# Output projection in a hybrid mixer kernel: from plain 128-token blocks to Strassen's seven products

## Chip, cores and metric

One core of a Trainium2 chip. The metric is the device time of one execution in microseconds (us); lower is better. Engines in the profile: PE is TensorE (PEld its weight loads), DVE is VectorE, ACT is ScalarE, POOL is GpSimd, SP is SyncE, which here only issues DMAs.

## What is computed

The reference is one layer of a diffusion backbone over 2,048 latent tokens and 256 context tokens with D_MODEL = 1024, all in fp32. Two token mixers (a bidirectional gated DeltaNet and a windowed attention) each give a 512-wide result per token, ya and yb. Then:

```
def _merge(ya, yb, ga, gb, w_proj_a, w_proj_b, w_out):
    y = jax.nn.sigmoid(ga) * (ya @ w_proj_a) + jax.nn.sigmoid(gb) * (yb @ w_proj_b)
    return y @ w_out
...
x = x + gate[:, None] * _merge(ya, yb, ga, gb, w_proj_a, w_proj_b, w_out)
```

The change is about the last product alone, y (2048 x 1024) by w_out (1024 x 1024), with its gated residual.

## The kernel before

**Products in three passes.** A matmul of the kernel works on fp32r tiles: a value is split into a high part (an ACT copy into an fp32r tile) and a low part (value minus high part, a subtraction on DVE or POOL). A product of two split operands is three matmuls, high x high, high x low and low x high, added up in PSUM. Every operand of every dense product thus costs one ACT operation and one subtraction.

**The stages before the end.** Input projections, convolutions, the DeltaNet's scan and the attention come first. `project(pool, wp, gi, ...)` (L1187 on) makes y for a group gi of 512 tokens: for each of 8 blocks of 128 columns two PSUM groups of 12 matmuls (L1198 to L1200) with ya and yb, an evaluation of the gate on DVE (L1206), a sum (L1208, on DVE for the last group, else on POOL), and a store of the block to the DRAM scratch `ysp[gi]`, transposed: [128 columns, k, 512 tokens]. The groups come in the order 1, 2, 0, 3. Groups 1, 2 and 0 run between pieces of the attention; group 3 runs alone after it. Its y tiles lie in the pool `proj`; the projection weights lie in the four 16 KB tiles of the pool hA (tags hh0, hl0, hh1, hl1).

**The output projection** (L1239 to L1303) takes half a group, 256 tokens, at a time: eight halves. `load_half` brings y in four pieces (L1249, issued on ACT's queue) and splits them on ACT (L1250) and DVE (L1251). w_out is loaded in 16 pieces of 128 x 512 (L1270) and split on ACT (L1271) and POOL (L1272). Its first NWO = 5 k slices have tiles in the pools p4r and p4 (opened when the attention's pools close, one at either end of the free space); the other three take the place of projection weights in hA, so they wait for `project` to end. For half 0 the four output blocks (2 token blocks x 2 column halves) are first accumulated over k = 0 to 4, then finished; later halves run block by block, 24 matmuls each. A block leaves PSUM in a DVE multiply by the gate row gbc (L1298); POOL (DVE for the last half) adds the residual x (L1299), and the rows are stored.

**What sets the order.** The program is written in sequence, and a scheduler orders each engine's instructions by priority (position in the program) as soon as they are ready in its own estimate of the time; on the chip every engine then runs its list in order. `tc.high_priority` moves the loads and splits for half 0 and for w_out ahead, to the priority of `project` of group 3. Tiles of a pool are given places in the order in which they are first asked for; a new tile on the place of an older one waits until that one's last user is done. [...]

**Pools and places.** Before the last stage the free space of a partition holds, from the low end, the attention's left pool (about 38 KB), `proj` (y high and y low in two buffers of 4 KB each, then two tb tiles of 2 KB, 20 KB in all), and at the high end the attention's right pool (46 KB). The last stage's p4 starts at the low end (56 KB) and p4r ends at the high end (44 KB).

Of the kernel before, what the change touches and what calls it, by code (L numbers as in the profile page):

```python
# [7 lines left out]
F32 = mybir.dt.float32  # L8
# [9 lines left out]
KT = D // 128  # L18
# [10 lines left out]
def f32(ap):  # L29
    return ap.bitcast(F32)  # L30
# [10 lines left out]
def _hybrid(ctx, tc, nc, V, S, G, T, ins, out, dbg, upto):  # L41
# [1197 lines left out]
    with tc.tile_pool(name="p4r", bufs=2, side="right", reuse_waits="tile") as pr4, \  # L1239
            tc.tile_pool(name="p4", bufs=2, reuse_waits="tile") as p4:  # L1240
        halves = [2 * gi + j for gi in (1, 2, 0, 3) for j in range(2)]

        def load_half(i):
            pool = pr4 if i % 2 == 0 else p4
            yh = pool.tile([128, KT, 256], F32R, name=f"yh{i % 2}", bufs=1)
            yl = pool.tile([128, KT, 256], F32R, name=f"yl{i % 2}", bufs=1)
            for k in range(0, KT, 2):
                yr = pr4.tile([128, 2, 256], F32, name="yq")
                adma(yr, ysp[halves[i] // 2][:, k:k + 2, halves[i] % 2 * 256:halves[i] % 2 * 256 + 256])  # L1249
                S.copy(yh[:, k:k + 2], yr)  # L1250
                V.tensor_tensor(yl[:, k:k + 2], yr, f32(yh[:, k:k + 2]), op=ALU.subtract)  # L1251
            return yh, yl

        woh, wol = [], []
        with tc.high_priority(tc.cur_priority - p_last):
            yy = load_half(0)
            for k in range(KT):
                if k < NWO:
                    pool = pr4 if k < 2 else p4
                    woh.append(pool.tile([128, D], F32R, name=f"woh{k}", bufs=1))  # L1260
                    wol.append(pool.tile([128, D], F32R, name=f"wol{k}", bufs=1))
                else:
                    if (k - NWO) % 2 == 0:
                        wo4 = hA.tile([128, 4, D], F32R, name="wo4", tag=("hh0", "hl0")[(k - NWO) // 2])
                    woh.append(wo4[:, (k - NWO) % 2 * 2])
                    wol.append(wo4[:, (k - NWO) % 2 * 2 + 1])
                for n in range(2):
                    ns = slice(n * 512, n * 512 + 512)
                    wr = pr4.tile([128, 512], F32, name="wor", bufs=4)
                    adma(wr, ins["w_out"][0, k * 128:(k + 1) * 128, ns])  # L1270
                    S.copy(woh[k][:, ns], wr)  # L1271
                    G.tensor_tensor(wol[k][:, ns], wr, f32(woh[k][:, ns]), op=ALU.subtract)  # L1272
        gbc = p4.tile([128, D], F32, name="gbc", bufs=1)
        dma(gbc, gsp.to_broadcast([128, D]))
        for i, hb in enumerate(halves):
            yh, yl = load_half(i) if i else yy
            tiles = [(tb, n, acc([128, 512], name="ops")) for tb in range(2) for n in range(2)]

            def products(tb, n, ps, ks):
                sl = slice(tb * 128, tb * 128 + 128)  # L1280
                ns = slice(n * 512, n * 512 + 512)
                for k in ks:
                    T.matmul(ps, lhsT=yh[:, k, sl], rhs=woh[k][:, ns], start=k == 0, stop=False)  # L1283
                    T.matmul(ps, lhsT=yh[:, k, sl], rhs=wol[k][:, ns], start=False, stop=False)  # L1284
                    T.matmul(ps, lhsT=yl[:, k, sl], rhs=woh[k][:, ns], start=False, stop=k == KT - 1)  # L1285

            if i == 0:
                for t in tiles:
                    products(*t, range(NWO))
# [59 lines left out]
```

## Time and profile before

| | |
|---|---|
| Median of 3 runs | 2045.72 us (2042.43 to 2046.54) |
| The profiled execution's own time | 2046.15 us |
| Its span, first to last instruction | 2044.3 us |
| Granted TensorE clock, mean | 0.988 |
| Output projection: first to last matmul | 1862.40 to 2039.93 us |
| DMA over the span | 333.12 MB, mean 163 GB/s |

The span is one profiled execution of the program; a line of it names the source line, the engine, the operation, the tiles written and read, and the count. "128x512" is partitions by elements. In a timeline the first two columns are start and duration in us, and "[1.15 <-DMA wor]" says that the engine was idle for 1.15 us before and what ended it; several instructions in a row are merged into one line with "x3". In lines by source the three numbers are the shortest, the median and the longest duration in ns. In the table of stretches each engine has its busy us and, in brackets, its instructions, and PEclk is the granted clock as a share of the full one. A line's second bar starts the idle time before the group.

### The profile page before, as it was taken

Reading aid. Unit: us, or ns where it says so; the run is one execution under the profiler, and the core shown is the slowest. Engines: PE = TensorE matmul, PEld = TensorE weight load, DVE = VectorE, ACT = ScalarE, POOL = GpSimd, SP = SyncE. Lnnn points to the kernel's source line nnn. Section 1 sums busy time; section 2 is a strip of 40 time slices with the busy share of each in tenths; the row PEclk is TensorE's granted clock in tenths of the full one; section 3 lists DMA queues with packets and bytes.
Section 4 is the critical chain, followed back from the end, with each engine's and each line's share of the span. In section 5 each row is a group of like instructions: output and inputs, shape, how many; then the busy total and the mean of one; then the engine's idle time right before and its main releaser. Section 6 shows DMA issues by size and latency. Waiting matters only on the chain. (4 is left out here: it accounts for less than half of the span.)

```text
span 2044.3 us, 32068 instructions
## 1 busy us (share of the span) xinstructions
PE 1966.8 (96%) x11043; PEld 1643.2 (80%) x11043; DVE 1421.5 (70%) x2715; ACT 760.4 (37%) x1927; POOL 742.9 (36%) x876
## 2 busy tenths in 40 slices
PE   6899999989999999999999999999989999999999
PEld 3888888778898677787788888878868888878887
DVE  6888766667766999999689655536577777753322
ACT  5655555544443211101122233325476556531100
POOL 2862211235553433224322234324256443442321
PEclk8999999999999999999999999999999999999999
DMA  7462236754447533437876787663456655355542
GB/s 256 141 166 85 89 97 165 188 149 155 147 136 197 154 109 111 132 98 220 201 218 205 221 244 214 185 207 116 129 165 204 185 167 158 120 174 189 185 144 93
DMA packets 375511, 333.12 MB, mean 163 GB/s; under 512 B 83832, under 2 KB 299184, under 8 KB 374708
## 3 DMA queue, kind: packets, MB, share of 16 engines
q1 hardware_dynamic: 347924, 288.59, 49.1%
q10 hardware_dynamic: 27424, 42.48, 5.9%
q8 instruction: 87, 1.43, 0.3%
q14 instruction: 76, 0.62, 0.1%
HBM read 220.28 MB, written 109.13 MB: 161 GB/s over the span
## 5 line engine op out<-in xcount | busy, mean ns | idle before, releaser
L523 PE MATMUL rps<-hh,wh 128*128 128x512 f32 x768 | 309.9, 404 | 10.1 <-DVE rt L811 5.2
L525 PE MATMUL rps<-hh,wl 128*128 128x512 f32 x768 | 310.3, 404 | 1.6 <-DVE wl L243 1.6
L524 PE MATMUL rps<-hl,wh 128*128 128x512 f32 x768 | 307.8, 401 | 0.0
L242 POOL TENSOR_SCALAR wh<-wr 128x512 fp32r<-128x512 f32 x120 | 104.7, 885 | 278.6 <-PE rps L524 105.8
L523 PEld LDWEIGHTS rps<-hh,wh 128*128 128x128 f32 x768 | 145.6, 190 | 47.1 <-POOL wh L242 4.9
L525 PEld LDWEIGHTS rps<-hh,wl 128*128 128x128 f32 x768 | 145.4, 189 | 35.1 <-DVE wl L243 2.4
L523 PE MATMUL lps<-hh,wh 128*128 128x512 f32 (+1 forms) x448 | 172.1, 384 | 0.3 <-ACT y L633 0.3
L524 PEld LDWEIGHTS rps<-hl,wh 128*128 128x128 f32 x768 | 145.8, 190 | 32.9
L525 PE MATMUL lps<-hh,wl 128*128 128x512 f32 (+1 forms) x448 | 171.1, 382 | 0.0
L524 PE MATMUL lps<-hl,wh 128*128 128x512 f32 (+1 forms) x448 | 171.1, 382 | 0.0
L562 DVE SCALAR_TENSOR_TENSOR cacc<-y,cw,cacc 128x512 f32<-128x512 f32 (+1 forms) x224 | 160.6, 739 | 14.3 <-ACT cacc L560 11.3
L809 ACT ACTIVATE rt<-rps 128x512 f32<-128x512 f32 x96 | 57.3, 597 | 287.5 <-PE rps L525 228.6
L909 DVE CUSTOM_DVE_ANT_0 pr<-sc,band,sk 128x640 f32<-128x640 f32 (+1 forms) x128 | 106.4, 863 | 42.5 <-PE sc L905 22.1
L937 DVE TENSOR_TENSOR pl<-pt,ph 128x512 fp32r<-128x512 f32 x156 | 105.0, 685 | 40.9 <-ACT ph L935 40.3
L935 ACT CAST ph<-pt 128x512 fp32r<-128x512 f32 x156 | 90.2, 585 | 111.7 <-PE pt L933 77.0
L748 DVE TENSOR_TENSOR N<-N,btmp 128x62 f32<-128x62 f32 (+30 forms) x124 | 123.7, 997 | 3.1
L746 DVE TENSOR_TENSOR btmp<-N 128x62 f32<-128x62 f32 (+30 forms) x124 | 119.2, 962 | 3.2
L919 POOL TENSOR_SCALAR pr<-pr,sm 128x640 f32<-128x640 f32 (+1 forms) x128 | 98.9, 793 | 57.1 <-DVE sm L917 44.5
L911 ACT ACTIVATE pr<-pr,sm 128x640 f32<-128x640 f32 (+1 forms) x128 | 104.0, 815 | 24.6 <-DVE sm L909 24.6
L1198 PE MATMUL pps<-yh,wph 128*128 128x512 f32 x256 | 105.1, 414 | 5.0 <-DVE tb L1206 2.0
L243 DVE TENSOR_TENSOR wl<-wr,wh 128x512 fp32r<-128x512 f32 x120 | 94.0, 796 | 18.1 <-POOL wh L242 17.9
L1199 PE MATMUL pps<-yl,wph 128*128 128x512 f32 x256 | 101.7, 397 | 0.9 <-DVE yl L1181 0.9
(301 smaller groups left out, 4925.9 us busy)
## 6 DMA issues: line engine op xcount, KB each, us to landing
wr<-in_w_in_dram SPq DMA_DIRECT2D x120, 256.0 KB
kw<-Ksp SPq DMA_DIRECT2D x28, 384.0 KB
x<-vsp SPq DMA_DIRECT2D x36, 256.0 KB
k<-ksp SPq DMA_DIRECT2D x34, 256.0 KB
kT<-kTsp SPq DMA_DIRECT2D x34, 256.0 KB
wm<-in_w_mod_dram SPq DMA_DIRECT2D x16, 512.0 KB
xt<-in_x_dram SPq DMA_DIRECT2D x16, 512.0 KB
dtl<-Dsp SPq DMA_DIRECT2D x32, 256.0 KB
```

The costliest lines, as they stand in the source:

```text
L242: G.tensor_scalar(wh[:, k:k + 4], wr, 1.0, 1.0, op0=ALU.mult, op1=ALU.mult)
L523: T.matmul(ps, lhsT=wh[:, k], rhs=xh[:, k], start=k == 0, stop=False)
L524: T.matmul(ps, lhsT=wh[:, k], rhs=xl[:, k], start=False, stop=False)
L525: T.matmul(ps, lhsT=wl[:, k], rhs=xh[:, k], start=False, stop=k == kt - 1)
L562: V.scalar_tensor_tensor(a, y[:, t:t + n], cw[:, m, t:t + 1], a, op0=ALU.mult, op1=ALU.add)
L746: V.tensor_tensor(tv, A[:, m + 1:, m].unsqueeze(2).to_broadcast([h1 + n, r, m]), A[:, m, 0:m].unsqueeze(1).to_broadcast([h1 + n, r, m]), o ...
L748: V.tensor_tensor(A[:, m + 1:, 0:m], A[:, m + 1:, 0:m], tv, op=ALU.add)
L909: V.tensor_tensor_reduce(s_, ps[:, o:768], band[:, b0:b0 + W + 256], -0.125, sk[:, 1, hd:hd + 1], ALU.add, ALU.min, sm[:, h, 1:2])
L911: S.activation(s_, s_, AF.Exp, scale=-1.0, bias=sm[:, h, 1:2], accum_out=sm[:, h, 2:3])
L937: V.tensor_tensor(pl, pt, f32(ph), op=ALU.subtract)
L1198: T.matmul(ps, lhsT=wh[:, k, ms], rhs=hs[k], start=k == 0, stop=False)
L1199: T.matmul(ps, lhsT=wh[:, k, ms], rhs=ls[k], start=False, stop=False)
```

## The change

w_out is cut into 2x2 blocks of 512 x 512 (B11, B12, B21, B22), and a unit of 256 tokens into 2x2 blocks of 128 tokens x 512 columns (a11, a12, a21, a22). Seven block products (Winograd's form of Strassen's method) replace eight:

- First half of a unit: p1 = a11 B11, p3 = S4 B22 with S4 = a12 - S2, p2 = a12 B21. Output block (0,0) is p1 + p2.
- Second half: p6 = S2 T2, p5 = S1 T1, p7 = S3 T3, p4 = a22 T4, with S1 = a21 + a22, S2 = S1 - a11, S3 = a11 - a21 and T1 to T4 sums and differences of w_out's blocks. The other three output blocks are sums of products.

The sums of operands are made in fp32 and split afterwards, so every summed operand has its own ACT copy and subtraction. A product is 4 k x 3 passes = 12 matmuls; it leaves PSUM by an ACT copy (p1, p3) or a DVE add. Units 0 to 3 run their first halves, which need only plain blocks of w_out, then the summed operands T1 to T4 are made in hA (where the projection weights were, behind `project`), then the four second halves follow, for which y is loaded again. Units 4 to 7 run whole, with one load. The gate's multiply and the residual's add move to POOL (DVE for the last unit), four of each for a unit. `plain_operands` and unit 0's first half have the high priority. Pool p4r now holds 84 KB, p4 24 KB.

The core of the diff (removed lines: the whole of the old stage; kept out: `store`, which multiplies by gbc, adds x and stores, and the pool's opening):

```diff
+        LATE = ("S1h", "S1l", "S2h", "S2l", "S3h", "S3l", "A4h", "A4l")
+        def raw_w(i, j, k, tag):
+            t = pr4.tile([128, 512], F32, name="wor", tag=tag)
+            adma(t, ins["w_out"][0, i * 512 + k * 128:i * 512 + k * 128 + 128, j * 512:j * 512 + 512])
+            return t
+        def split(pool, src, name, eng, bufs=1, tags=None):
+            hl_ = [pool.tile(list(src.shape), F32R, name=name + x, tag=name + x, bufs=bufs) for x in "hl"]
+            S.copy(hl_[0], src)
+            eng.tensor_tensor(hl_[1], src, f32(hl_[0]), op=ALU.subtract)
+            return hl_
+        def plain_operands():
+            n = 0
+            for nm, i, j in (("B11", 0, 0), ("B22", 1, 1), ("B21", 1, 0)):
+                W[nm] = [pr4.tile([128, 4, 512], F32R, name=nm + x) for x in "hl"]
+                for k in range(4):
+                    wr = raw_w(i, j, k, LATE[n % 8])
+                    n += 1
+                    S.copy(W[nm][0][:, k], wr)
+                    G.tensor_tensor(W[nm][1][:, k], wr, f32(W[nm][0][:, k]), op=ALU.subtract)
+        def summed_operands():
+            for nm, tag in (("T2", "hh0"), ("T3", "hl0"), ("T1", "hh1"), ("T4", "hl1")):
+                t = hA.tile([128, 2, 4, 512], F32R, name=nm, tag=tag)
+                W[nm] = [t[:, 0], t[:, 1]]
+            for k in range(4):
+                b11, b12, b21, b22 = (raw_w(i, j, k, LATE[k % 2 * 4 + i * 2 + j]) for i in range(2) for j in range(2))
+                V.tensor_tensor(b11, b12, b11, op=ALU.subtract)
+                V.tensor_tensor(b12, b22, b12, op=ALU.subtract)
+                G.tensor_tensor(b22, b22, b11, op=ALU.subtract)
+                G.tensor_tensor(b21, b21, b22, op=ALU.subtract)
+                for nm, t, eng in (("T2", b22, V), ("T1", b11, V), ("T3", b12, V), ("T4", b21, G)):
+                    S.copy(W[nm][0][:, k], t)
+                    eng.tensor_tensor(W[nm][1][:, k], t, f32(W[nm][0][:, k]), op=ALU.subtract)
+        def load_u(u):
...
+            yr = pr4.tile([128, KT, 256], F32, name="yr")
+            for k in range(0, KT, 4):
+                adma(yr[:, k:k + 4], ysp[gi][:, k:k + 4, o:o + 256])
...
+        def product(ps, hl_, nm):
+            (h, l), (wh, wl) = hl_, W[nm]
+            for k in range(4):
+                T.matmul(ps, lhsT=h[:, k], rhs=wh[:, k], start=k == 0, stop=False)
+                T.matmul(ps, lhsT=h[:, k], rhs=wl[:, k], start=False, stop=False)
+                T.matmul(ps, lhsT=l[:, k], rhs=wh[:, k], start=False, stop=k == 3)
...
+        def operands2(a11, a21, a22, s1, s2):
+            S1 = split(pr4, s1, "S1", V)
+            if s2 is None:
+                s2 = sum_("s2", s1, a11, ALU.subtract, V)
+            S2 = split(pr4, s2, "S2", V)
+            S3 = split(pr4, sum_("s3", a11, a21, ALU.subtract, G), "S3", V)
+            return S1, S2, S3, split(pr4, a22, "A4", V)
+        def first_half(u, whole=False):
+            ((a11, a12), (a21, a22)), a1 = load_u(u)
+            A1 = split(p4 if u % 2 else pr4, a1, f"A1{u % 2}", V)
+            s1 = sum_("s1", a21, a22, ALU.add, G)
+            if whole:
+                s2 = sum_("s2", s1, a11, ALU.subtract, V)
+                rest = operands2(a11, a21, a22, s1, s2)
+            else:
+                s2, rest = s1, None
+                G.tensor_tensor(s2, s1, a11, op=ALU.subtract)
+            V.tensor_tensor(s2, a12, s2, op=ALU.subtract)
+            S4 = split(pr4, s2, "S4", V)
...
+            product(p1, [t[:, 0:4] for t in A1], "B11")
...
+            S.copy(x1, p1)
+            product(p3, S4, "B22")
+            S.copy(t, p3)
+            product(p2, [t_[:, 4:8] for t_ in A1], "B21")
+            V.tensor_tensor(og, p2, x1, op=ALU.add)
+            store(u, 0, 0, og)
...
+        def second_half(u):
...
+            if rest is None:
+                ((a11, a12), (a21, a22)), _ = load_u(u)
+                rest = operands2(a11, a21, a22, sum_("s1", a21, a22, ALU.add, V), None)
+            S1, S2, S3, A4 = rest
...
+            product(p6, S2, "T2")
+            V.tensor_tensor(x1, p6, x1, op=ALU.add)
+            G.tensor_tensor(t, x1, t, op=ALU.add)
+            product(p5, S1, "T1")
+            V.tensor_tensor(t, p5, t, op=ALU.add)
+            store(u, 0, 1, t)
+            product(p7, S3, "T3")
+            V.tensor_tensor(x1, p7, x1, op=ALU.add)
...
+            V.tensor_tensor(u3, p5, x1, op=ALU.add)
+            store(u, 1, 1, u3)
+            product(p4_, A4, "T4")
+            V.tensor_tensor(x1, p4_, x1, op=ALU.add)
+            store(u, 1, 0, x1)
         with tc.high_priority(tc.cur_priority - p_last):
-            yy = load_half(0)
...
+            plain_operands()
+            first_half(0)
+        EARLY = 4
+        for u in range(1, EARLY):
+            first_half(u)
+        summed_operands()
+        for u in range(EARLY):
+            second_half(u)
+        for u in range(EARLY, 8):
+            first_half(u, True)
+            second_half(u)
```

89 lines of the change are left out of this document (30 added, 59 removed).

## Prediction

> **What bounds the kernel now.** I read the page, then the stage that the change touches: its busy times, its first and last instructions, its waits, and the engines that would get the new work.
>
> ```profile
> span 2044.3 us, 32068 instructions
> PE 1966.8 (96%) x11043; PEld 1643.2 (80%) x11043; DVE 1421.5 (70%) x2715; ACT 760.4 (37%) x1927; POOL 742.9 (36%) x876
> ```
>
> The shares are means over all stages. The output projection (L1283 to L1285) begins at 1862.40 us. Busy times of its stretch:
>
> ```profile
> core 0: us, PE busy (x) PEld busy (x) DVE busy (x) ACT busy (x) POOL busy (x), PEclk, DMA share, GB/s
> 1862.40:2040.00 177.60, 177.52 (x769) 143.85 (x767) 52.09 (x69) 21.45 (x36) 49.00 (x36) 1.00 0.46 150
> ```
>
> The timeline of PE, its first and last matmul of this stage, and that of DVE behind it:
>
> ```profile
> 1862.40 0.39 PE L1283 MATMUL ops<-woh,yh 128*128 128x512 f32 x1
> ...
> 2039.53 0.40 PE L1285 MATMUL ops<-wo,yl 128*128 128x512 f32 x1
> ```
>
> ```profile
> 2039.96 0.69 DVE L1298 TENSOR_TENSOR og<-ops,gbc 128x512 f32<-128x512 f32 x1 [4.14 <-PE ops L1285]
> 2040.69 0.69 DVE L1299 TENSOR_TENSOR xr<-og,xr 128x512 f32<-128x512 f32 x1
> ```
>
> PE never idles here and the granted clock is 1.00: PE sets this stage. The code issues 16 blocks of 128 tokens x 2 column halves x 8 k x 3 passes = 768 matmuls, in 1862.40 to 2039.93, so 0.2312 us each. Behind the last come two DVE operations, done at 2041.38, and 2.9 us to the span's end for the store. POOL is busy 49 of 177.6 us and DVE 52: this is the room that the change spends.
>
> **The change: what it removes.** Each unit of 256 tokens makes 7 products of 4 k x 3 passes = 84 matmuls where there were 96. 8 x 84 = 672, 96 fewer: 96 x 0.2312 = 22.2 us, all of it on the path, if PE stays full.
>
> **What it adds on POOL and DVE.** The durations, by line, of the operations that exist already:
>
> ```profile
> L1272 POOL TENSOR_TENSOR wol<-wor,woh x10: 1287/1300/1737, 1823.3 to 1875.7; 128x512 fp32r<-128x512 f32 x10
> L1251 DVE TENSOR_TENSOR yl<-yq,yh x32: 679/692/1789, 1820.8 to 2003.1; 128x512 fp32r<-128x512 f32 x32
> L1298 DVE TENSOR_TENSOR og<-ops,gbc x32: 675/692/693, 1887.5 to 2040.0; 128x512 f32<-128x512 f32 x32
> L1250 ACT CAST yh<-yq x32: 615/620/627, 1820.1 to 2002.4; 128x512 fp32r<-128x512 f32 x32
> ```
>
> The maxima matter: a DVE subtraction of two SBUF tiles (L1251) is 0.69 us or up to 1.79; the multiply whose first input is in PSUM (L1298) is never above 0.693. The timelines of POOL and of DVE show why, at two places:
>
> ```profile
> 1833.53 3.79 POOL L1272 TENSOR_TENSOR wol<-wor,woh 128x512 fp32r<-128x512 f32 x3
> ...
> 1888.24 4.32 POOL L1299 TENSOR_TENSOR xr<-og,xr 128x512 f32<-128x512 f32 x3 [1.85 <-DVE og L1298]
> ```
>
> ```profile
> 1835.99 1.87 DVE L1208 TENSOR_TENSOR ta<-ta,tb 128x512 f32<-128x512 f32 x1
> ...
> 1890.17 2.93 DVE L1251 TENSOR_TENSOR yl<-yq,yh 128x512 fp32r<-128x512 f32 x2
> ```
>
> The DVE add of 1835.99 ends 0.54 us after the three POOL operations do (1837.32). At 1888.24 three POOL operations and two DVE ones take until 1893.10, 4.86 us; the three alone are 3 x 1.29 = 3.87, so each DVE operation adds 0.50. Thus a POOL operation on 128x512 and a DVE operation with two SBUF inputs run one after the other: I count 1.29 us of shared time for the one, 0.50 for the other (a 1,024-wide one twice that), and none for a DVE operation that reads PSUM.
>
> The count, from the code. POOL: 12 low parts of B11, B22, B21; 12 for the summed operands (two differences and T4's low part, four times); in each first half of units 0 to 3 the sums s1, s2 and a store's multiply and add, 4; in each second half s3, one sum of products and three stores, 8. Units 4 to 7 have 11 each, the last fewer, as its stores go to DVE. DVE with two SBUF inputs, in 512-wide pieces: 4 in a first half (A1 counts two), 20 for the summed operands, 6 in a second half of units 0 to 3, 9 in a whole unit 4 to 7.
>
> Units 0 to 3 with all operands: POOL 12 + 16 + 12 + 32 = 72, DVE 16 + 20 + 24 = 60: 72 x 1.29 + 60 x 0.50 = 122.9 us. PE has 4 x 84 x 0.2312 = 77.7 us for them. Here PE is no longer the bound. A whole unit 4 to 7: 11 x 1.29 + 9 x 0.50 = 18.7 us against 19.4 on PE: PE again, barely.
>
> The bounds of this price: nothing (the two overlap fully), or every operation at its full 1.29 and 0.69. I take 0.50 since the stretch at 1888.24 is the only one with both kinds queued in a row. [...]
>
> **Where this can start.** By the code's sizes, the pool p4r grows from 44 to 84 KB a partition and now reaches below the attention's right pool (46 KB) into the space of project's own tiles. In the order of declaration B11's low part, its four raw tiles (tags S1h to S2l) and B22 lie there. Such a wait shows in the waits of before, for yh1 of p4, which lies in that space as well; and the timeline of ACT has the price of a raw tile, issue to cast:
>
> ```profile
> ACT yh L1250 <- PE pps L1200: 27.8, 1, 27.8
> ```
>
> ```profile
> 1878.05 0.33 ACTq L1270 DMA_DIRECT2D wor<-in_w_out_dram  x1
> ...
> 1881.16 0.62 ACT L1271 CAST wo<-wor 128x512 fp32r<-128x512 f32 x1 [1.15 <-DMA wor<-in_w_out_dram]
> ```
>
> So B11's raw tiles load when project's last matmuls have read y: the first buffer six matmuls before 1862.40, at 1861.0, its cast 3.1 us later at 1864.1, POOL's first low part at 1864.7. In before this cost nothing, as the operands of 48 matmuls (k 0 to 3 of four blocks) were split by 1837.32; now PE idles from 1862.40. Behind the waiting DMA issues on ACT's queue are unit 0's copies; before it, units 0 and 1 can do 4 POOL and 7 DVE pieces: 4 x 1.29 + 7 x 0.50 = 8.7 us.
>
> **The sum.** 1864.7 + 122.9 - 8.7 = 1978.9 for units 0 to 3. Two things of opposite sign are left out: shared time that no queue can use while it waits for PE or a DMA, and unit 3's last stores, which can slide behind unit 4. Units 4 to 7 at PE's pace: 4 x 19.4 = 77.7, to 2056.6. The tail has three DVE operations for two (0.73 + 0.69 + 0.69 = 2.1) and the store's 2.9: 2061.6 us of span. The profiled execution took 2046.15 us for its span of 2044.3, 1.85 more, and the median of the runs, 2045.72, is 0.43 less than that: 2063 us.
>
> Costed at nothing: ACT (per unit 1.1 for the wide cast and 7 x 0.62 = 5.4 of 19.4 us; in the queue order a cast can stand behind one that waits for PE); 12 loads of 1 MB where there were 8, with DMA engines 0.46 busy. But yr is single: in second halves 1 to 3 the next load waits for the last cast of the one before. That is 1.3 for the last split, some 4 for 1 MB (an estimate from the 3.1 for a raw tile of 256 KB) and 2.6 for two differences and a split, in the 11.1 us of 48 matmuls: covered while the shared time sets the pace. PE's own clock is the other cover. The timeline of PE, and the busy times behind it:
>
> ```profile
> 683.79 0.47 PE L523 MATMUL rps<-hh,wh 128*128 128x512 f32 x1 [1.90 <-DVE rt L811]
> ```
>
> ```profile
> 684.80:688.20 3.40, 3.40 (x8) 2.72 (x9) 3.33 (x5) 0.00 (x0) 1.07 (x1) 0.50 0.66 204
> ```
>
> A gap of 1.90 us was followed by 3.4 us at half clock, 1.7 us of PE time lost. Units 0 to 3 will have such gaps, but there PE has 122.9 - 77.7 = 45 us to spare, so between 0 and, for four of them on the path, 7 us; I take 0. [...]
>
> **Rivals.** (1) *The two engines overlap after all*, because the queues' order seldom brings the two kinds together. Then POOL alone paces units 0 to 3: (72 - 4) x 1.29 = 87.7 from 1864.7 gives 1952.4, + 77.7 + 5.0 = 2035.1, a time of 2036.5: faster. It decides if DVE stays near 0.69 us where POOL is busy. For it: the median of L1251 is 0.69. Against: both places above. (2) *All is hidden*: 1862.4 + 672 x 0.2312 + 5.0 = 2022.8, a time of 2024. Against: POOL's 87.7 us alone exceed PE's 77.7. (3) *The raw tiles come early*, if the buffers lie otherwise: POOL's 12 low parts (15.5 us) and the 2.3 us of the start fall before 1862.4: 2063 - 17.8 = 2045, no change. The wait of 27.8 us speaks against it. (4) *The exclusion costs full durations*: 72 x 1.29 + 60 x 0.69 = 134.3, less 10.0, to 1989.0; whole units at 14.2 + 6.2 = 20.4, 81.6; + 5.0 = 2075.6, a time of 2077, and with the clock's 7 us 2084. For it: a POOL operation that met a DVE one took up to 1.74 us instead of 1.29. Against: the 0.50 of the stretch at 1888.24. [...]
>
> **How the numbers follow.** Forecast 0.52, (1) 0.15, (2) 0.05, (3) 0.10, (4) 0.18. Time 2063 us. A measurement of this kernel tells about 0.2%, 4.1 us, from no change. Faster: (1) and (2), 0.20; same: most of (3), 0.07; slower: 0.73. The range of 2036 to 2084 leaves out (2), about half of (1), and some 0.05 above; the forecast's own is 2052 to 2074.
>
> **What would show it.** In the profile after: 672 matmuls from L-lines of product; PE idle for about 2 us behind 1862; PE busy near 65 to 75% until about 1979, then near full; POOL and DVE together near the whole of that stretch; DVE subtractions with a mean of over 1 us, those from PSUM still at 0.69. The forecast is wrong if units 0 to 3 end before 1960, or if PE still idles much in units 5 to 7.

## The result and the profile after

The changed kernel takes 2092.23 us (median; 2088.28 to 2093.39), the kernel before beside it 2044.08 us: ratio 1.0229, 95% interval 1.0217 to 1.0242. It is 48 us slower; the forecast was 17 us slower. The page of the profiled execution:

```profile
span 2091.2 us, 32163 instructions
PE 1962.5 (94%) x10947; PEld 1637.5 (78%) x10947; DVE 1514.1 (72%) x2791; ACT 789.7 (38%) x1971; POOL 849.8 (41%) x940
```

There are 96 fewer matmuls, as the code says, yet PE's share has gone down and the span up: the stage waits. Busy times by stretch of the last stage, after:

```profile
core 0: us, PE busy (x) PEld busy (x) DVE busy (x) ACT busy (x) POOL busy (x), PEclk, DMA share, GB/s
...
1862.00:1900.00 38.00, 13.38 (x39) 9.48 (x40) 23.00 (x18) 16.69 (x27) 32.98 (x22) 0.66 0.74 242
1900.00:1940.00 40.00, 26.85 (x87) 20.09 (x88) 23.16 (x19) 10.30 (x16) 25.78 (x17) 0.80 0.30 99
1940.00:1980.00 40.00, 35.62 (x144) 28.48 (x144) 24.14 (x29) 7.73 (x13) 24.35 (x17) 0.93 0.41 137
1980.00:2020.00 40.00, 30.76 (x122) 24.12 (x121) 25.84 (x28) 8.55 (x13) 34.40 (x23) 0.91 0.57 191
2020.00:2060.00 40.00, 40.00 (x177) 32.95 (x176) 25.34 (x27) 9.12 (x15) 28.88 (x19) 1.00 0.43 144
```

Where before had one row with PE at 177.52 of 177.60, PE now has 13 of the first 38 us and is full only from 2020 on. The clock column has fallen with it: seven waits of PE of 3.3 us and more lie in this stage, and each had half clock (granted clock 0.50) at its end or within 0.3 us of it; of two waits of 2.4 to 2.5 us one was followed by it (the one ahead of 1938.24; 0.50 from 1938.80 to 1942.10) and one was not (ahead of 1987.38; 1.00 from 1987.30 to 1991.00). The timeline of PE at the start shows a wait and the half clock:

```profile
1860.64 0.40 PE L1200 MATMUL pps<-yh,wpl 128*128 128x512 f32 x1
1875.49 0.79 PE L1295 MATMUL p<-B11h,A10h 128*128 128x512 f32 x1 [14.45 <-ACT A10h L1254]
...
1878.32 0.63 PE L1296 MATMUL p<-B11l,A10h 128*128 128x512 f32 x1
1878.74 0.63 PE L1297 MATMUL p<-B11h,A10l 128*128 128x512 f32 x1
...
1888.02 0.80 PE L1295 MATMUL p<-B22h,S4h 128*128 128x512 f32 x1 [6.57 <-ACT S4h L1254]
```

Project ends at 1861.04, the first product comes 14.45 us later, runs with 0.42 us from matmul to matmul instead of 0.23, and ends at 1881.45; then PE waits again, 6.57 us for S4. ACT's timeline says why A10 is late:

```profile
1859.67 3.19 ACTq L1248 DMA_DIRECT2D wor<-in_w_out_dram  x5
1862.96 0.62 ACT L1267 CAST B11h<-wor 128x512 fp32r<-128x512 f32 x1 [38.10 <-DVE ta L1208]
...
1867.65 0.39 ACTq L1289 DMA_DIRECT2D yr<-ysp  x1
...
1874.39 1.04 ACT L1254 CAST A10h<-yr 128x1024 fp32r<-128x1024 f32 x1 [0.91 <-DMA yr<-ysp]
```

Unit 0's y, complete in DRAM long before, is asked for only at 1867.65, behind the raw weight loads and the casts that wait for project's tiles. POOL's first low part of B11 is at 1863.65 (forecast 1864.7), and neither POOL nor DVE has done anything for unit 0 by then. The groups of DVE, then of POOL, from project's end on:

```profile
L1283 DVE TENSOR_TENSOR T<-wor,T 128x512 fp32r<-128x512 f32 x12 | 17.6, 1489 | 1.4 <-ACT T L1282 1.4
L1337 DVE TENSOR_TENSOR s<-yr,s 128x512 f32<-128x512 f32 x8 | 12.1, 1507 | 7.4 <-POOL s L1336 7.3
L1348 DVE TENSOR_TENSOR og<-p,hold 128x512 f32<-128x512 f32 x8 | 5.5, 688 | 21.2 <-PE p L1297 21.2
```

```profile
L1314 POOL TENSOR_TENSOR s<-yr 128x512 f32<-128x512 f32 x16 | 25.7, 1603 | 14.0 <-DMA yr<-ysp 8.4 <-DVE S1l L1255 4.3 <-DVE S4l L1255 1.3
```

The exclusion is there as argued: DVE operations with two SBUF inputs have means of 1.49 and 1.51 us (the other such groups of 512 elements, of four operations and more, lie between 0.82 and 1.58), the one that reads PSUM 0.688, and this POOL group's mean is 1.60 where an operation alone took 1.29.

From PE's timeline: units 0 to 3 end at 1998.57 (forecast 1978.9), unit 4 takes 29.0 us to its last matmul at 2027.54, units 5 to 7 have 19.3 us each (forecast 19.4), the last matmul ends at 2085.31, and 5.9 us follow (forecast 5.0).

One execution of the kernel "low parts on DVE" below was disturbed (2471.99 us at a granted clock of 0.715) and is left out of its ratio; as its profile is of that execution, this kernel has no figures from a trace.

### The profile page after: what moved, and what is told of

Read it like the earlier page. It is cut to its first block, busy times and chain, and to the rows that moved or that the text cites. A ratio compares the mean times of both kernels' runs of the same rounds, so it can differ in the third digit from the quotient of the medians.

```text
span 2091.2 us, 32163 instructions
## 1 busy us (share of the span) xinstructions
PE 1962.5 (94%) x10947; PEld 1637.5 (78%) x10947; DVE 1514.1 (72%) x2791; ACT 789.7 (38%) x1971; POOL 849.8 (41%) x940
```

## The experiments

**Theory A:** two terms that add: the exclusion of POOL and DVE, and a late start. **Rival Q:** the start's queue order alone is the cost, and PE's pace would follow. **Rival C:** POOL and DVE are simply full. The table has all kernels; the times of the first product and of the last matmul's end, and the time between them at granted clock 0.5 (gaps within it included), are from the PE timeline and the clock of each profile. Ratios are to the kernel before, run beside each (medians of 2043.8 to 2047.5), with the 95% interval. The last four columns are of one execution of each kernel, the profiled one, which can lie some us from the kernel's median; the farthest is "+ POOL's queue", profiled at 2068.50 us with a median of 2060.19.

| Kernel | median us | ratio | first product | last end | between | half clock |
|---|---|---|---|---|---|---|
| after | 2092.23 | 1.0229 [1.0217, 1.0242] | 1875.5 | 2085.3 | 209.8 | 42.8 |
| y first | 2093.44 | 1.0232 [1.0207, 1.0257] | 1875.2 | 2089.6 | 214.4 | 46.8 |
| placement 1 | 2087.56 | 1.0200 [1.0175, 1.0224] | 1867.9 | 2075.5 | 207.6 | 42.9 |
| all on DVE | 2065.26 | 1.0105 [1.0065, 1.0144] | 1876.1 | 2059.7 | 183.6 | 27.3 |
| fills, both | 2089.22 | 1.0213 [1.0188, 1.0238] | 1894.0 | 2086.2 | 192.3 | 32.0 |
| fills, own tile | 2099.24 (one run) | | 1899.2 | 2092.2 | 193.1 | 31.8 |
| fills for the gate | 2086.12 | 1.0192 [1.0175, 1.0209] | 1872.6 | 2076.4 | 203.8 | 43.7 |
| placement 2 | 2078.60 (one run) | | 1862.8 | 2071.6 | 208.8 | 44.0 |
| placement 2, DVE | 2058.53 | 1.0053 [1.0034, 1.0072] | 1866.2 | 2051.5 | 185.3 | 25.4 |
| + 24 matmuls | 2061.97 | 1.0067 [1.0044, 1.0090] | 1866.9 | 2051.3 | 184.3 | 27.1 |
| + y in two places | 2050.93 | 1.0020 [1.0008, 1.0032] | 1870.6 | 2045.4 | 174.9 | 20.1 |
| + T in pairs | 2054.83 | 1.0043 [1.0028, 1.0059] | 1872.7 | 2048.7 | 176.0 | 15.7 |
| + POOL's queue | 2060.19 | 1.0062 [1.0045, 1.0079] | 1872.5 | 2061.5 | 189.0 | 27.3 |
| both cures | 2061.28 | 1.0077 [1.0063, 1.0091] | 1876.3 | 2054.2 | 177.9 | 21.4 |
| all at once, DVE | 2063.33 | 1.0086 [1.0072, 1.0099] | 1865.3 | 2056.1 | 190.8 | 26.9 |
| all at once, POOL | 2086.62 | 1.0194 [1.0174, 1.0215] | 1865.7 | 2080.3 | 214.6 | 52.8 |
| low parts on POOL | 2062.80 | 1.0079 [1.0059, 1.0099] | 1864.7 | 2051.9 | 187.2 | 29.8 |
| low parts on DVE | 2057.28 | 1.0040 [1.0024, 1.0055] | | | | |

### The start

*y first.* Unit 0's load stands ahead of the weights.

```diff
...
+            y0 = load_u(0)
             plain_operands()
-            first_half(0)
+            first_half(0, y=y0)
```

> Unit 0's load of y is issued before the loads and the splitting of the weights; nothing else changes. After: 2092. Theory A (VectorE's pieces with two inputs in SBUF and GpSimd's pieces can't run at the same time, and their summed time sets the pace of units 0 to 3; the late start is a term of its own): the gap of 14.85 us between project's last matmul and the first product shrinks by up to 10 us, since the y tile need not stand behind the loads on ScalarE's queue any more, and the exclusive pieces move up by as much: 2080 to 2086. Rival Q (the order on ScalarE's queue at the start is the main cost of the change, all else would follow at TensorE's pace): unit 0 starts within 5 us of project's end and most of the idle time of TensorE (some 55 us in all) goes: under 2065. Rival N (the weights' splits set the start, not y): within 3 us of 2092.

Nothing gained, as the third reading of the expectation (N, the weights' splits set the start) had it; Rival Q falls in this form. ACT's timeline:

```profile
1851.66 5.83 ACTq L1289 DMA_DIRECT2D yr<-ysp  x2
1863.65 9.90 ACTq L1248 DMA_DIRECT2D wor<-in_w_out_dram  x8
1873.59 1.04 ACT L1254 CAST A10h<-yr 128x1024 fp32r<-128x1024 f32 x1 [43.31 <-DMA wor<-in_w_out_dram]
```

y is asked for 16 us earlier, but its cast now stands behind eight raw loads that wait for project's tiles. Project's last matmul ended at 1865.25 in this execution, 4.2 us later than in after, so the gap was 10.0 us and the first product no earlier.

*Placement 1.* The tags of p4r are asked for once in another order, and the raw blocks of B11, B22 and B21 take six of the early ones.

```diff
+        for tag, shape in (("yr", [128, KT, 256]), ("S4h", [128, 512]), ... ("A10l", [128, 1024])):
+            pr4.tile(shape, F32R, name=f"{tag}_", tag=tag)
+        EARLY_RAW = ("S1h", "S1l", "S2h", "S2l", "A4h", "A4l")
...
-                    wr = raw_w(i, j, k, LATE[n % 8])
+                    wr = raw_w(i, j, k, EARLY_RAW[n % 6])
```

> The stage's tiles are declared in another order, so that y's tile, the operands S4 and A4h, B11 and B22 and the tiles into which the first weight blocks are loaded lie in space that is free once the attention is over, and the operands needed later lie on project's tiles. Same instructions, and the same order on each queue. Theory A: the loads of B11 and B22 and their splits run under project, where TensorE has its own work, and about eight of GpSimd's low parts (1.3 us each, some 10 us) and the gap of 14.85 us before the first product go; the exclusive time of units 0 to 3 stays: 2062 to 2072. Rival Q (the order of ScalarE's queue): as the y load's early issue alone gives. Rival N (project has no slack on GpSimd and VectorE, so that the early pieces delay it): project ends later by as much as the start gains, within 5 us of 2092.

The first product came 7.6 us earlier and the time fell by less than forecast. B11's casts still waited, until 1859.84, behind project's last addition (of "ta"); by the sizes of the tiles B11's high part still shared 448 bytes with project's last tile.

*Placement 2.* That overlap is gone, and four raw blocks use the tiles of xr.

```diff
...
+                    wr = raw_w(i, j, k, "xr" if nm == "B22" else LATE[k])
...
+                b11, b12, b21, b22 = (raw_w(i, j, k, LATE[i * 2 + j]) for i in range(2) for j in range(2))
```

> The placement again, without the overlap that was left: in the first placement B11's high half still shared 448 bytes with project's last tile. Now y, S4, B11, B22, A10 and the raw weight tiles of the first eight blocks (four of them in the tiles of the stores' residual) lie outside project's tiles, and the raw blocks of the summed operands use four tiles only; elementwise work on the engines of after. Theory A: unit 0's pieces and B11 and B22 with their eight low parts run under project, so the gap before the first product (14.85 us in after) shrinks to under 5 us and the exclusive time left after project falls by about 10 to 15 us; from there units 0 to 3 go at the pace of the two excluding engines as before: 2062 to 2075. Rival N (the early pieces slow project): project ends later and the time stays at 2080 to 2092.

2078.6 in its one run, somewhat over the expected range: the gap ahead of the first product is 5 us instead of 14.5, but the stretch behind it is as long as before (208.8 for 209.8). The start is a term of its own, of some 13 us by this run, and does nothing for the rest. Only places were changed here, not the order on a queue.

### The exclusion

*All on DVE.* One line, `G = V`, ahead of the stage.

> Every elementwise operation that this stage has on GpSimd goes to VectorE; nothing else changes. Theory A: without GpSimd's pieces VectorE's two-input subtractions go back from some 1.5 us to about 0.5 to 0.7 us, and all of the stage's elementwise work together is some 160 us on one engine, about what TensorE has in matmuls (155 us); with the late start of the first product that remains: 2050 to 2075, faster than 2092. Rival C (the two engines are independent and both are simply full): one engine gets what two had, 33 us or more of GpSimd's busy time per 40 us comes on top of VectorE's 23 to 25: far slower, over 2150.

27 us faster than after, with the first product no earlier (1876.1); Rival C falls, since one engine doing the work of both would have been slower. The same groups as above, of this kernel (its lines are one further on):

```profile
L1284 DVE TENSOR_TENSOR T<-wor,T 128x512 fp32r<-128x512 f32 x16 | 10.8, 685 | 0.0
L1338 DVE TENSOR_TENSOR s<-yr,s 128x512 f32<-128x512 f32 x8 | 5.5, 684 | 0.0
L1349 DVE TENSOR_TENSOR og<-p,hold 128x512 f32<-128x512 f32 x8 | 5.5, 684 | 2.4 <-PE p L1298 2.4
```

Every group of eight and more DVE operations on 512 elements, with two SBUF inputs or with PSUM, has a mean of 0.68 to 0.69 us once POOL is silent. POOL's help cost more than it gave.

The gain is not the exclusion alone. An operation that moves is itself shorter on DVE (0.68 us for POOL's 1.29 to 1.60), and POOL's queue goes out of the chain. After has a place that shows this, ahead of S4 of unit 3; POOL's timeline, then DVE's:

```profile
1930.78 1.29 POOL L1306 TENSOR_TENSOR og<-og,gbc 128x512 f32<-128x512 f32 x1 [7.21 <-DVE og L1348]
1932.02 2.26 POOL L1314 TENSOR_TENSOR s<-yr 128x512 f32<-128x512 f32 x1
1934.25 1.28 POOL L1307 TENSOR_TENSOR xr<-og,xr 128x512 f32<-128x512 f32 x1
1935.49 1.26 POOL L1336 TENSOR_TENSOR s<-s,yr 128x512 f32<-128x512 f32 x1
```

```profile
1936.79 0.69 DVE L1337 TENSOR_TENSOR s<-yr,s 128x512 f32<-128x512 f32 x1 [3.64 <-POOL s L1336]
```

Unit 2's store stands before and between the two sums of unit 3, and DVE, which runs nothing meanwhile, waits 3.64 us for the second; PE's wait of 2.44 us for S4 follows. How the 27 us divide between exclusion, length and queue no run says. The next kernels show the exclusion by itself.

*Fills in place of POOL's arithmetic*, at first for both operations of a store: the kernel leaves out the gate and the residual for units 0 to 6 and writes zeros in five fills.

```diff
-            (V if last else G).tensor_tensor(t, t, gbc[:, cs_], op=ALU.mult)
-            (V if last else G).tensor_tensor(xr, t, xr, op=ALU.add)
...
+            else:
+                for x in (t, t, xr, xr, xr):
+                    G.memset(x, 0.0)
```

> This kernel leaves out the gate's multiplication and the residual's addition at the stores of units 0 to 6 and writes zeros in their place: the two GpSimd operations of a store become five fills of a 128x512 tile, about the same time of GpSimd, which read nothing. [...] Rival C (GpSimd is full, whatever it does): within 5 us of 2092, VectorE's subtractions as before. [...]

The total moved by 3 us only, where the exclusion was to give 10 to 25, but not because POOL is full: the fills of xr depend on no product, 40 of them ran under project, the residual's loads and the stores went with them (317 GB/s in 1862 to 1900, where after has 242), and the first product came 18 us late. From it to the end the kernel is 17.5 us shorter than after (part of which can come from transfers done before and stores that wait for nothing), and in its groups of DVE the subtractions of A4 (0.680 us) and S3 (0.688) are back at the time of one alone. Of after, then of this kernel:

```profile
L1255 DVE TENSOR_TENSOR A4l<-yr,A4h 128x512 fp32r<-128x512 f32 x8 | 11.1, 1382 | 0.0
```

```profile
L1255 DVE TENSOR_TENSOR A4l<-yr,A4h 128x512 fp32r<-128x512 f32 x8 | 5.4, 680 | 0.0
```

To mend the start, all five fills went to the product's own tile:

> As the first kernel with fills, and again without the gate's multiplication and the residual's addition at the stores of units 0 to 6, but all five fills of a store go to the product's own tile, so that they can't run ahead under project as the fills of the residual's tile did there (40 of them, and the first product came 18 us later). Theory A: first product at about 1875 as in after, the stretch from there to the last matmul about 192 us as with the first fills (after: 210), the time 2070 to 2078. Rival C (GpSimd's busy time as such): the stretch stays near 210 and the time near 2092.

A miss in the total: the residual now passed through its tile without any wait, and its transfers crowded the start still more (DMA share 0.99 in 1862 to 1900, where after has 0.74). The stretch behind it is 193.1, as expected, in its one run. Then the gate alone was replaced, by three fills, with the residual's addition kept:

> This kernel leaves out the gate's multiplication at the stores of units 0 to 6: three fills of 128x512 of GpSimd stand in its place (1.6 us, as long as the multiplication took), and the residual's addition stays, so that the residual's loads and the stores wait as they do in after and nothing runs ahead under project, which spoiled the start in both kernels with fills before. Theory A: 28 of the two-input operations of GpSimd that exclude VectorE's go, with no change of GpSimd's time: first product at about 1875 as in after, and the rest shorter by half of what both kernels with fills showed (17 us), so 2081 to 2086. Rival C (GpSimd's time as such): 2089 to 2095.

2086.1, the upper end of A's range; the stretch is 6.0 us shorter (8.5 expected). In this kernel's groups DVE's s<-yr,s has come down from 1507 to 1136 ns beside fills that hold POOL as long as the multiplication did:

```profile
L1341 DVE TENSOR_TENSOR s<-yr,s 128x512 f32<-128x512 f32 x8 | 9.1, 1136 | 4.2 <-POOL s L1340 4.1
```

```profile
L1310 POOL MEMSET hold<- 128x512 f32 x42 | 22.1, 527 | 7.3 <-DVE hold L1368 5.0 <-DVE hold L1376 1.6
```

So it is what POOL does, not that POOL is busy: fills in place of 28 of its two-input operations, with the same POOL time and the same waits, are worth 6.0 us.

### Mending both, and what is left

*Placement 2 and all on DVE.*

> The same placement, and every elementwise operation of the stage on VectorE. Theory A (exclusion and the late start are two terms that add): everything on VectorE gave 2065 with a gap of 18 us before the first product and 12 us of half clock; without that gap and with 12 low parts and unit 0's pieces under project: 2038 to 2052, about the time before the change (2044). Rival S (VectorE is now the bound, and what is won at the start is waited for later): 2055 to 2065.

2058.5, above A's range and inside its rival's: against placement 2 alone 20 us faster, so POOL's share is paid for at any start; against all on DVE only 7 us, as 7.2 us of the 18 us of gap ahead of the first product remained. The stretch behind it is no shorter (185.3 for 183.6). PE's timeline has later gaps too, 1.19 us ahead of T2 and, ahead of T1:

```profile
1917.69 0.80 PE L1303 MATMUL p<-T,S1h 128*128 128x512 f32 x1 [4.38 <-ACT S1h L1262]
```

*y in two places:* in the second halves of units 1 and 3 y is loaded into the tiles of A1.

```diff
+            if alt is not None:
+                ys = [alt[0].tile([128, 4, 256], F32, name="yr2", tag=alt[1] + x) for x in "hl"]
...
-                ((a11, a12), (a21, a22)), _ = load_u(u)
+                ((a11, a12), (a21, a22)), _ = load_u(u, {1: (pr4, "A10"), 3: (p4, "A11")}.get(u))
```

> The second placement with VectorE, and in the second halves of units 1 and 3 y is loaded into the tiles that A1 has left, so that the next unit's y need not wait for the last reader of the one before. Theory: the gaps ahead of units 3 and 4 (2.9 and 3.9 us) and the half clock behind them (3.4 and 6.8 us of window, 1.7 and 3.4 lost) come from y's reload through one tile: without them 2047 to 2053. Rival S (VectorE is the bound there): under 3 us of gain, 2055 to 2060.

As the theory had it: the stretch is 10.4 us shorter, and once T2 and T1 are through, PE is never short of work:

```profile
1940.00:1980.00 40.00, 40.00 (x178) 33.14 (x177) 38.22 (x64) 9.75 (x15) 0.00 (x0) 1.00 0.52 172
```

DVE has 38.22 of 40 us beside it. What is left lies ahead: 7.6 us of gap at the start, 2.3 ahead of unit 2's S4, 3.8 ahead of T2 and 4.9 ahead of T1, each with half clock at its end or soon behind it (20.1 us at granted clock 0.5 in all). ACT's timeline has the last: S1's cast stands behind the casts of the next T, which wait for raw blocks.

```profile
1920.72 1.34 ACT L1290 CAST T<-wor 128x512 fp32r<-128x512 f32 x2 [2.53 <-DVE wor L1286]
1921.97 0.61 ACT L1262 CAST S1h<-s 128x512 fp32r<-128x512 f32 x1
```

This is the best version of the change, and still 1.0020 of the kernel before (1.0008 to 1.0032).

*24 matmuls more*, on project's operands, ahead of the first product of placement 2 with DVE:

```diff
+        if gi == 3:
+            ps = acc([128, 512], name="fill")
+            for n in range(24):
+                T.matmul(ps, lhsT=wp[0][0][:, 0, ms], rhs=yy[0][0][3], start=n == 0, stop=n == 23)
```

> The second placement with VectorE, and 24 matmuls more between project's last matmul and the first product, on project's operands into a sum that nobody reads. They take about 24 x 0.2312 = 5.5 us of a gap that was 7.6 us. If the gap is what brings TensorE to half clock in the first products (granted clock 0.5 from 1864.2 to 1871.0 there, 6.8 us that cost 3.4), these windows go and the time falls by about 3 us, 2053 to 2057; if half clock comes for another reason, or the fills delay the first product, it stays at 2057 to 2062.

No gain (the gap without them was 7.20 us, not the 7.6 of the expectation). PE's timeline, and the busy times behind the gap that was left:

```profile
1858.51 5.78 PE L1213 MATMUL fill<-yh,wph 128*128 128x512 f32 x24
1866.94 0.80 PE L1307 MATMUL p<-B11h,A10h 128*128 128x512 f32 x1 [2.66 <-ACT A10h L1266]
```

```profile
1866.70:1873.50 6.80, 6.17 (x14) 4.38 (x15) 4.52 (x7) 2.81 (x6) 0.00 (x0) 0.50 0.91 285
```

What was left of the gap, 2.66 us, was followed by 6.8 us at half clock all the same, and the first product came 8.3 us behind project instead of 7.2. Whether a closed gap would have kept the clock the run does not say.

*T in pairs:* the summed operands' raw blocks in two sets of four tiles again, `LATE[k % 2 * 4 + i * 2 + j]`. *POOL's queue:* the same, raw blocks loaded by `nc.gpsimd.dma_start`.

> All on VectorE, second placement, y in two places, and the raw blocks of the summed operands again in two sets of four tiles as in after (the version ahead had one set). If T1's lateness (gaps of 4.2 and 5.3 us and the half clock behind them, 10 us of window) comes from the single set of tiles, T is ready in time: 2037 to 2045, under the kernel before (2047). If VectorE is the bound in units 0 to 3, T gets no earlier: 2048 to 2054.

> The same, with the raw blocks of the weights loaded by GpSimd's queue instead of ScalarE's; GpSimd has no arithmetic in this stage. If the gap of 8 us before the first product comes from the order on ScalarE's queue (loads that wait there for transfers of project, with casts behind them), the first product follows project within 3 us and the half clock there goes: 2027 to 2040. If the start hangs on VectorE or on the transfers themselves, it stays where the first kernel of this pair is, within 3 us of it.

In the first the wait ahead of S1 was gone (after a gap of 3.8 us for S2, which ends at 1925.19, only one of 1.19 us is left), and the total got worse all the same, with a gap of 12.1 us at the start. ACT's timeline:

```profile
1865.48 6.09 ACTq L1256 DMA_DIRECT2D wor<-in_w_out_dram  x6
1871.61 1.04 ACT L1262 CAST A10h<-yr 128x1024 fp32r<-128x1024 f32 x1 [5.53 <-DMA wor<-in_w_out_dram]
```

Raw loads, T's first ones among them, stand ahead of A10's cast, and the low parts of B22, whose high parts were cast by 1857, come on DVE at 1861.98, behind project's last addition. With POOL's queue the raw blocks were asked for at 1823 and B22 was cast at 1836, and the first product followed project without a gap, only to wait 4.3 us for the low parts of B11 a little later. But project itself ended at 1872.6, 11.6 us later than in after, in an execution that was 8.3 us longer than this kernel's median. ACT's waits name project's own load, and DVE's low parts again came (at 1874.01) behind project's last addition:

```profile
ACT B11h L1275 <- DMA tb<-gbsp: 25.1, 1, 25.1
```

Whether the early loads slow project by their transfers is suggested by this profile and not shown. What it does show is that the raw loads need not wait for their tiles: on POOL's queue all eight were issued by 1827.65, one behind the other, while with the same places on ACT's queue (y in two places) the last four went at 1849.62, 1854.41, 1856.57 and 1857.65, each by the profile 0.02 us after a transfer of project's own (ta, tb or ysp) had landed, with B22's casts behind them.

*Both cures:* y first and the two sets of tiles, loaded by SyncE's queue.

> All of the stage on VectorE, second placement, y in two places, the summed operands' raw blocks in two sets of tiles and on SyncE's queue, y of unit 0 loaded first. If the two waits are independent: first product within 5 us of project, T1 in time, 2032 to 2042, under the kernel before. If one is paid with the other, because VectorE and ScalarE take the early pieces of T in front of units 1 to 3: 2048 to 2058.

The second outcome, and 3 us over its range: T in time, first product 10 us behind a project that ended 5 us late, as ACT's queue stood at the loads of four raw blocks:

```profile
1861.77 10.78 ACTq L1256 DMA_DIRECT2D wor<-in_w_out_dram  x4
```

*All at once*, first with everything on DVE, then with POOL's share back: y, B22, B11 and unit 0's first half get the priority of project's first group, T's raw blocks go by SyncE's queue, and y has two places.

> All on VectorE with the second placement, and more of what the trace of that kernel shows waiting: unit 0's y, the plain operands and unit 0's first half are ordered ahead of project's last three groups, y is loaded first; the summed operands' raw blocks go by SyncE's queue; in the second halves of units 1 and 3 y lies in the tiles that A1 has left, so that y can be loaded before the unit ahead is done. Theory A (what is left over TensorE's 155 us is start, exclusion, y's reload and half clock, and each can be taken away by itself): 2030 to 2046, under the kernel before (2044). Rival S (VectorE's own time in units 0 to 3 is the bound by now): 2050 to 2058, no better than the second placement with VectorE.

> The same kernel with GpSimd's share of the elementwise work left where after has it. Theory A: with start and reload mended, what stays against the version all on VectorE is the exclusion: 15 to 25 us slower than that one, 2050 to 2070. Rival Q (start and queue order were all): within 5 us of the version all on VectorE, since GpSimd takes work from VectorE.

The first missed, slower than both of its ranges: the first product came at 1865.3 and the stretch behind it grew to 190.8. That T's raw blocks, which share tiles with the residuals of stores, came late is how I read the order of the tiles; no run showed it. The second is over its range as well, but the difference of the pair holds: 23.3 us for POOL's share, the third pair of this kind.

*Low parts of B11 and B22 on POOL or on DVE*, with T ahead of unit 2 in program order:

> All of the stage on VectorE but the eight low parts of B11 and B22, which GpSimd makes under project; y, B11 and B22 ordered ahead of project's last groups; the summed operands' raw blocks by SyncE's queue in two sets of tiles, and built after unit 1's first half in program order; y in two places. If the start's order is the last term: first product within 4 us of project's last matmul, first halves at 13 us each and less, 2030 to 2044, under the kernel before (2047). If the wait only moves (to y's own load, or to T), 2045 to 2056.

> The same with these eight low parts on VectorE. If VectorE's order behind project's last additions is what holds the first product: some 4 to 8 us slower than the kernel with them on GpSimd. If it is the loads: within 2 us of it.

Against both expectations, POOL's version is the slower one, by 5.5 us in the medians (the intervals of the ratios do not overlap), and over both of its ranges, though its first product came within 4 us of project as hoped (3.47). The low parts were meant to run under project, but their casts came at 1860.94, behind loads on ACT's queue. So POOL worked from 1861.63 to 1875.25, and DVE's operations for unit 0 beside it took about two and a half times their 0.69 us:

```profile
1863.39 1.77 DVE L1327 TENSOR_TENSOR s<-yr 128x512 f32<-128x512 f32 x1
1865.20 1.65 DVE L1349 TENSOR_TENSOR s<-s,yr 128x512 f32<-128x512 f32 x1
```

No version beats the kernel before. What the runs leave open is whether a start without a gap can be had at all: the wait moved each time to another of the queues that run in order (ACT's loads and casts, DVE behind project's last addition, T behind y), and what makes ACT's loads wait for project's transfers was not tried by itself.

## Why the prediction was wrong

Direction and mechanism were right, the size was not: 29.6 us of span too low (2061.6 for 2091.2). Units 0 to 3 are 19.7 of them, unit 4 is 9.5, units 5 to 7 give 0.4 back, and the tail is 0.9.

- **PE's pace and the matmuls saved** held: 672 matmuls, 19.3 us a unit once PE is full.
- **The step that failed** is "1864.7 + 122.9 - 8.7 = 1978.9": it lets the two engines work without a break. Laid over each other, the records of POOL's operations and DVE's two-input operations cover 113.3 of the 136.6 us from 1862.0 to 1998.6; in 23.3 us neither ran. The prediction named that term, "shared time that no queue can use while it waits for PE or a DMA", and set it to nothing against stores that slide.
- **What filled the 23.3 us.** Four pauses make up 17.2 of them: 1.9 us from 1914.42, 5.2 from 1925.55, 5.2 from 1938.91 and 4.8 from 1952.12. Each lies behind the issue of the next y into its one tile (1910.49, 1924.31, 1937.67, 1950.86). ACT's timeline at the second:

```profile
1924.31 0.99 ACTq L1289 DMA_DIRECT2D yr<-ysp  x2
1929.85 1.05 ACT L1254 CAST A11h<-yr 128x1024 fp32r<-128x1024 f32 x1 [5.03 <-DMA yr<-ysp]
```

  So y's single tile, "covered while the shared time sets the pace", was in the pace of units 0 to 3 already, and a load took some 5.5 us where the prediction estimated 4. At about the end of the three longer pauses a product also left PE, which was late and at half clock itself; which of the two held the engines was not separated.
- **The price of the exclusion** held nearly. 66 of POOL's operations and 62 two-input pieces of DVE lie in that stretch, 116 us by the forecast's prices for 113.3 measured. That this is close to the forecast's own 114.2 is luck: the 8.7 us ahead of project's end were not done, and seven of POOL's operations of units 0 to 3 (9.0 us) slid behind 1998.57.
- **The work ahead of project's end** failed: "before it, units 0 and 1 can do 4 POOL and 7 DVE pieces" (8.7 us). They did none. The argument looked at where the raw tiles lie, rightly, and not at the order of ACT's queue, where y stands behind them. But y first alone gained nothing; places alone gave 13.6 us in the one run of placement 2.
- **Unit 4**, which the forecast has at PE's pace: its S4 came 5.6 us late. Its y could be asked for only at 1991.26, behind unit 3's last split of that tile, and was there at 1996.85 (cast of A10); the sums and splits behind it then met POOL's, a DVE addition taking 1.77 us, until S4's cast at 2007.73. PE's timeline:

```profile
2008.40 0.79 PE L1295 MATMUL p<-B22h,S4h 128*128 128x512 f32 x1 [5.59 <-ACT S4h L1254]
```

  So it was reload and exclusion together. With everything on DVE, two places took 0.33% off (1.0053 to 1.0020), 6.8 us.
- **The clock, "I take 0", at most 7 us**: at half clock PE is busy for 31.6 us of the stage, about half of which, 15.8 us, is lost (an estimate from 0.42 us a matmul there for 0.23). How much of it was on the path was not separated; PE's spare time of 45 us, on which the 0 rested, was spent by the waits themselves. The price from "a gap of 1.90 us" was weak as well: in after's profile the same gap, ahead of the same matmul at 683.81, has full clock behind it.
- **Rivals.** The overlap of the two engines (1) is refuted by DVE's means and by the fills. Rival (4) has the nearest time, 2077 to 2084, for a wrong reason: by its prices the operations in the stretch would take 127.9 us, and the records cover 113.3. Rival (3) is about placement 2: 13.6 us for the 17.8 given.
- **The signs**: DVE's means, PSUM at 0.69, PE at 64% until 1980 (75.85 of 118 us in the table of stretches) and full in units 5 to 7 came; "PE idle for about 2 us behind 1862" did not (14.45), nor POOL and DVE "together near the whole of that stretch" (83%).

The change does not pay even with the exclusion and y's reload gone: in the best version the 22.2 us of matmuls saved go for 7.6 us at the start, 12.6 of gaps behind it (8.7 of them ahead of T2 and T1), and some 7.5 lost to the half clock, at which PE is busy for 15.0 us. Before needed none of this, as its operands were plain, and 48 matmuls' worth lay ready when project ended.

## What to carry to other kernels

A trade of matmuls for sums of operands is a trade of a steady engine for a chain through three: count the chain's waits, not only the busy time of its engines, and expect the sum of busy times to be a floor. Work given to GpSimd beside VectorE's two-input operations was not parallel work here: taking all of it away from GpSimd gained 20 to 27 us. A buffer that exists once, reloaded by the stage itself, belongs in the sum as a wait. At a border between two stages follow each new operand through every queue that it passes, by place and by order, since one operation that waits for the old stage holds all behind it.

## What the runs showed of the hardware

- Beside GpSimd's additions a 128x512 VectorE operation with two SBUF inputs took up to 1.84 us in after (means of its groups of four and more 0.82 to 1.58), and 0.682 to 0.688 (means of groups of eight and more) where everything was on VectorE. Where fills stood in for the stores' arithmetic a split took 0.680 (after: 1.382). One group of GpSimd's sums averaged 1.60 in after, where an operation alone took 1.29. What makes the two slow each other no run shows.
- TensorE ran its products at granted clock 0.50 for 6.8 us after a gap of 2.66 us (24 matmuls more), and for 3.4 us after one of 1.90 us (before).
- The length of a gap alone did not tell what followed. Behind the gap of 1.90 us ahead of the same matmul the granted clock from 684.80 to 688.20 was 0.50 in before, with 8 matmuls, and 1.00 in after, with 15 (columns as in the tables above):

```profile
684.80:688.20 3.40, 3.40 (x15) 2.76 (x16) 3.33 (x5) 0.00 (x0) 1.11 (x1) 1.00 0.66 206
```

  What decided between the two was not shown.
